# Post-norm pages by halves, kept activation sums, and two more units of the down projection by seven products

## The chip, the core and the metric

The kernel runs on one core of a Trainium2 chip. Its time is the device time of one execution in microseconds. Times of single executions are given as the median of three; the profile is of one more execution, with its own time.

## What is computed

One layer of an encoder block over 256 positions of width 2048, in 32-bit floats. The part that the change touches is the second sub-layer's way out, `@ w_down` and the norm behind it, and the gate that follows:

```python
def conv_glu(hn, w_up, conv_w, conv_b, w_down):
    up = hn @ w_up
    gate, val = jnp.split(up, 2, axis=-1)
    gate = dwconv_centred(gate, conv_w, conv_b)
    return (jax.nn.gelu(gate, approximate=True) * val) @ w_down
...
        mix = jnp.concatenate([y_ssd, y_pool], axis=-1) @ w_out[i]
        h = h + rmsnorm(mix, mix_norm_post[i])
        hn = rmsnorm(h, ffn_norm_pre[i])
        ff = conv_glu(hn, w_ffn_up[i], ffn_conv_w[i], ffn_conv_b[i], w_ffn_down[i])
        h = h + rmsnorm(ff, ffn_norm_post[i])
        gate = jax.nn.sigmoid(rmsnorm(h, ple_norm_pre[i]) @ w_ple_gate[i])
        h = h + rmsnorm(gate * (p[i] @ w_ple[i]), ple_norm_post[i])
```

`w_down` is 5632 x 2048, `w_out` and `w_gate` are 2048 x 2048.

## The kernel before

**Precision.** Every 32-bit operand is split into a high part (a rounding copy on ScalarE, L153) and a low part (the difference, on VectorE, L154); `split` does it for weights, `hid_split` (L962) for the activations of the down projection. A product of two numbers is three matmuls: high by high, high by low and low by high, all 128 x 128 by 128 x 512 (`mm`, L90).

**Stages in order.** The input projections and the state-space and pooling mixers (to about 196 us), the output projection ("wo", to 284 us), a small embedding product ("ple"), the up projection ("ga" and "va", to 785 us), the down projection ("dn", to 1006.6 us), the second half of the embedding product, and the gate ("gt", to the end).

**The sub-layer.** `sublayer` (L854) works "wo" and "dn". It goes through two halves of 1024 output columns. In each, `token_major` (L319) goes through units of two row blocks of 128 of the weight; "dn" has 44 blocks, so 22 units a half. Unit u has the blocks 2u and 2u+1, and tiles are named by the even block and the half: `dn120` is unit 10 of the second half, `dn134` unit 17, `dn18` unit 4, `dn122` unit 11. At the end of a half the accumulators are multiplied by the gain and put aside in two pages `mg` (named `dnm`), one for each 128 positions, taken at the start of the sub-layer; behind the second half they are scaled by the row norm and added to `h` (L883).

**Ordinary and fast units.** An ordinary unit loads 1 MB of weight (`raw`), makes two splits of 1024 columns and issues 24 matmuls. A unit in `dn_fast` is worked by `seven_products` (L269): block products in Strassen's manner, 7 in place of 8, so 21 matmuls. For these it needs sums of weight blocks (a page `t` of 128 x 2048, made by the four additions of `add_blocks`, L263) and sums of activations (`hid_sums`, L1087). Its splits are called `a` (512 columns), `b` (1024, both of the raw weight), `d` and `c` (1024 each, of the page of sums). The products that belong to several output blocks go to separate accumulators (`dn1s`, `dns`), and `combine` (L297) adds them to the main ones (`dna`) one unit after the last fast one; `acc[1][1]`, whose accumulator the text calls dna11_1, is the last of them.

**Where the sums come from.** The weight sums are made ahead, during the up projection: `block_sums` (L227) fetches a raw page (SyncE), adds (VectorE), and stores it to device memory (POOL's queue). A fast unit then loads the page of sums (1 MB, `dn1..t<-dns`) and the last three quarters of the raw weight (768 KB). If no sums are there for a unit, `seven_products` loads the full 1 MB and adds in place, with the splits `a` and `b` ahead. Activation sums of 13 units are made ahead too (`dn_stored`) and loaded by POOL; those of the others are made on the spot in each half: four 128-column operations, a cast, and a 512-column subtraction (`pair_sums`, L818).

**Buffers.** 13 pages of 128 x 2048, 3 raw buffers of the same size, 5 high and 5 low split tiles of 1024 columns, 3 `mid` tiles, 2 activation splits. Loads wait on SyncE for their buffer, and SyncE issues them in its program's order.

**Order.** Only the up projection has its order written out (`in_order`). Elsewhere a scheduler orders the instructions of each engine, so an edit moves instructions that it doesn't name. At unit 11 of the second half, `first` (L1110) loads and splits the gate's first weight (`gtf`, `gtfh`, `gtfl`); at its end `ple_parts` and `back` load the embedding weight and `h`.

Of the kernel before, what the change touches and what calls it, by code (L numbers as in the profile page):

```python
# [11 lines left out]
F32 = mybir.dt.float32  # L12
F32R = mybir.dt.float32r
AF = mybir.ActivationFunctionType
ALU = mybir.AluOpType
ORDERED = (mybir.EngineType.Activation, mybir.EngineType.DVE, mybir.EngineType.SP)

P = 128
# [35 lines left out]
def build(nc, a, out):  # L54
# [3 lines left out]
    w_down, w_gate, w_ple = a["w_down"], a["w_gate"], a["w_ple_"]  # L58
    out = out[0]

    with tile.TileContext(nc) as tc, \
# [9 lines left out]
        def ins(r):  # L71
            return getattr(r, "ins", r)

        def page(name, dtype=F32):
            return gp.tile([P, 2048], dtype, tag="pg", bufs=13, name=name)

        def mid(name, dtype=F32):
            return gp.tile([P, 1024], dtype, tag="mid", bufs=3, name=name)

        def tiny(name, n=2):  # L80
            return sp.tile([P, n], F32, tag="tiny", bufs=40, name=name)
# [35 lines left out]
        def load(dst, src, ahead=False):  # L117

            with tc.issue_after(last["dma"]) if last and not ahead else nullcontext():
                return ins(nc.sync.dma_start(dst, src))  # L120
# [21 lines left out]
        def split(name, src, nel, cuts=()):  # L142

            if name in ready:
                return ready.pop(name)
            if name in spare:
                hi, lo = spare.pop(name)
            else:
                hi = wp.tile([P, 1056], F32R, tag="whi", bufs=5, name=f"{name}h")
                lo = wp.tile([P, 1056], F32R, tag="wlo", bufs=5, name=f"{name}l")  # L150
            for c0, c1 in zip((0, *cuts), (*cuts, nel)):
                s = slice(c0, c1)
                last["act"] = ins(nc.scalar.copy(hi[:, s], src[:, s]))  # L153
                last["dve"] = ins(nc.vector.tensor_sub(lo[:, s], src[:, s], hi[:, s].bitcast(F32)))  # L154
            return hi, lo

        def raw(name, src=None):
            r = wp.tile([P, 2048], F32, tag="raw", bufs=3, name=name)
            if src is not None:
                last["dma"] = load(r, src, True)  # L160
            return r
# [98 lines left out]
            nc.gpsimd.dma_start(t, r)  # L260
            sums_["wo", c * 1024, k] = t, False

        def add_blocks(r):  # L263

            v = r.rearrange("p (b c) -> p b c", b=4)
            for i, j in ((1, 0), (0, 3), (3, 1), (2, 3)):
                nc.vector.tensor_add(v[:, i], v[:, i], v[:, j])  # L267

        def seven_products(name, stage, w, k0, c0, a_, acc, alt, start, stop):  # L269

            if (stage, c0, k0) in sums_:
                r = raw(f"{name}r")
                last["dma"] = load(r[:, 512:], w[c0 // 1024, k0 // 2][:, 512:], True)
                t, held = sums_[stage, c0, k0]
                if not held:
                    t = page(f"{name}t")
                    last["dma"] = load(t, sums_[stage, c0, k0][0], True)
            else:  # L280
                r = t = raw(f"{name}r", w[c0 // 1024, k0 // 2])
            b11 = split(f"{name}a", r[:, 512:1024], 512)
            b2 = split(f"{name}b", r[:, 1024:], 1024)
            if r is t:
                add_blocks(r)
            t42 = split(f"{name}d", t[:, 1024:], 1024)
            t31 = split(f"{name}c", t[:, :1024], 1024)

            for x, (wh, wl), c, o, own in (
                    ("a11", b11, 0, alt[0], True), ("a12", b2, 0, acc[0][0], False), ("a22", t42, 0, acc[1][0], False),  # L290
                    ("s4", b2, 512, acc[0][1], False), ("s2", t42, 512, alt[3], True), ("s1", t31, 512, alt[1], True),
                    ("s3", t31, 0, alt[2], True)):
                xh, xl = a_[x]
                for q, (xx, ww) in enumerate(((xh, wh), (xh, wl), (xl, wh))):
                    mm(o, xx, ww[:, c:c + 512], own and start and q == 0, own and stop and q == 2)
# [175 lines left out]
        for u in range(0, NK, 2):  # L471
            r = [wp.tile([P, 2048], F32, tag="raw", bufs=3, name=f"dtur{u}") if u else r0, page(f"dtur{u + 1}")]
            for j in range(2):
                k = u + j
# [17 lines left out]
            for j in range(2):  # L492
                k = u + j
                with tc.issue_after(front[0]), tc.issue_after(front[1]):
                    wh, wl = split(f"dtu{k}", r[j][:, :1056], 1056, ((352, 704), (704,), (352,))[k] if k < 3 else ())
                if k == 8:
                    half = last["act"], last["dve"]
# [50 lines left out]
        for t in range(2):  # L548
# [3 lines left out]
                                    op0=ALU.mult)  # L552
# [229 lines left out]
        for t in range(2):  # L782
# [13 lines left out]
            r = rms(f"yn{t}", [ss], rz[t][:, 1:2], n=2)  # L796
# [56 lines left out]

        def sublayer(name, w, ks, get, gain, h, vnext, panel=Panel, fast=((), ()), sums=None, at=(), row=None, then=()):  # L854

            mg = [page(f"{name}m{t}") for t in range(2)]
            sq = [[], []]
            for half in range(2):

                alt = main(f"{name}s{half}") if fast[half] and half == 0 else []  # L860
                acc = [main(f"{name}a{half}{t}") for t in range(2)]
                if fast[half]:
                    alt += main(f"{name}s{half}") if half else []
                token_major(f"{name}{half}", w, half * 1024, ks, get, acc, 1, fast[half], alt, sums, at if half else ())
                for t in range(2):
                    for n in range(2):
                        q = tiny(f"{name}q{t}{half}{n}", 1)
                        junk = sp.tile([P, 512], F32, tag="junk", bufs=1, name=f"{name}j{t}{half}{n}")
                        c = slice(half * 1024 + n * 512, half * 1024 + (n + 1) * 512)
                        b = acc[t][n]  # L870
                        if row:
                            nc.scalar.activation(junk, b, AF.Square, scale=row[t], accum_out=q)
                            nc.vector.scalar_tensor_tensor(mg[t][:, c], b, row[t], gain[:, c], op0=ALU.mult, op1=ALU.mult)
                        else:
                            nc.scalar.activation(junk, b, AF.Square, accum_out=q)
                            nc.vector.tensor_mul(mg[t][:, c], b, gain[:, c])
                        sq[t].append(q)
            r = [rms(f"{name}{t}", sq[t], 1.0 / D) for t in range(2)]
            pan = panel(f"{name}x")
            for c in range(4):  # L880
                s = slice(c * 512, (c + 1) * 512)
                for t in range(2):
                    nc.vector.scalar_tensor_tensor(h[t][:, s], mg[t][:, s], r[t], h[t][:, s],  # L883
                                                   op0=ALU.mult, op1=ALU.add)
                panel_part(f"{name}x", pan, h, vnext, 4 * c, 4 * c + 4)
                if c in then:
                    then[c]()
            return pan
# [15 lines left out]
        h = [page(f"h{t}") for t in range(2)]  # L904
# [30 lines left out]
        for t in range(2):  # L935
            h_kept.append(dp.tile([P, D], F32, tag=f"h{t}", bufs=1, name=f"h_kept{t}"))
        pl_kept = dp.tile([P, D], F32, tag="pl", bufs=1, name="pl_kept")

        dn_fast, gt_fast = ((2, 3, 4, 5, 7, 8, 9, 10, 11, 12, 13, 14, 15, 16, 17, 18, 19), (2, 3, 4, 5, 7, 8, 9, 11, 12, 13, 14, 15, 16, 18, 19)), ((4, 5, 6), (1, 2))

        dn_stored = (2, 3, 5, 7, 8, 10, 11, 13, 14, 16, 17, 18, 19)
        gt_ks = list(range(NK)), [0, 1, 8, 9, 10, 11, 2, 3, 4, 5, 6, 7, 12, 13, 14, 15]
        which = [("dn", w_down, c * 1024, 2 * u) for c in range(2) for u in dn_fast[c]] + \
            [("gt", w_gate, c * 1024, gt_ks[c][2 * u]) for c in range(2) for u in gt_fast[c]]
        jobs_at = [[] for _ in range(NPIECES)]

# [3 lines left out]
        for i, w_ in enumerate(which[2:] + which[:2]):  # L950
            fetch, add, store = block_sums(*w_, i >= len(which) - 2)
            n = 46 * i // 10 + 4
# [4 lines left out]
        def hid_part(k):  # L957
            return hid[k // 8][:, (k % 8) * L:(k % 8 + 2) * L]
# [12 lines left out]
        def hid_sums_of(k, s, o):  # L971
            return pair_sums(f"he{k}", s, o, *(hid_part(k)[:, i * P:(i + 1) * P] for i in range(4)))
# [69 lines left out]
        row = norms_row()  # L1042
        with in_order():
            for _ in range(5):
                next_part()
            for n in range(NPIECES):
                s, v, i = blocks[n // 4]
# [32 lines left out]
        def hid_get(k):  # L1080
# [3 lines left out]
                hcache[k0], hcache[k0 + 1] = get_hid(k0), get_hid(k0 + 1)  # L1084
            return hcache[k]

        def hid_sums(k):  # L1087

            (h1, l1), (h2, l2) = get_hid(k), get_hid(k + 1)
            o = mid(f"hd{k}", F32R)  # L1090
            if k in kept:
                nc.gpsimd.dma_start(o.bitcast(F32), kept[k])
                d = sums_in(o)
            else:
                d = hid_sums_of(k, sp.tile([P, 512], F32, tag="junk", bufs=1, name=f"hs{k}"), o)
            return dict(d, a11=(h1[:, :P], l1[:, :P]), a12=(h2[:, :P], l2[:, :P]), a22=(h2[:, P:], l2[:, P:]))

        def ple_parts():
# [73 lines left out]
        for half in range(2):  # L1172
# [12 lines left out]
            for t in range(2):  # L1185
                for n, (o, c0) in enumerate(columns(acc[t])):
                    c1 = c0 + o.shape[-1]
                    c = slice(half * 1024 + c0, half * 1024 + c1)

                    th = mid(f"gth{half}{t}{n}")  # L1190
                    v = th[:, :c1 - c0]
                    end = half == t == 1 and c1 == 1024
                    if end:
# [3 lines left out]
                                                   op0=ALU.add, op1=ALU.mult)  # L1197
# [85 lines left out]
```

## Time and profile before

| | us |
|---|---|
| median of three executions | 1112.9 (1112.57 to 1112.93) |
| the profiled execution | 1113.11 |
| its span in the profile | 1111.3 |
| down, second half, from unit 1 to the end | 900.71 to 1006.56 |
| mean granted clock of TensorE | 0.998 of full speed |

An execution's time has 1.8 us that the span does not hold. Rows of a timeline read: start, duration, engine, line, operation, output <- inputs, shape, count, and in brackets an idle time before it with what ended it. PE is TensorE, DVE is VectorE, ACT is ScalarE, POOL is GpSimd, and SP is SyncE. Durations of neighbouring records on one engine overlap, so the cost of one is read from start to start. Rows of the transfers read: output <- input, queue, count, size, us from issue to landing.

### The profile page before, as it was taken

Reading aid. Unit: us, or ns where it says so; the run is one execution under the profiler, and the core shown is the slowest. Engines: PE = TensorE matmul, PEld = TensorE weight load, DVE = VectorE, ACT = ScalarE, POOL = GpSimd, SP = SyncE. Lnnn points to the kernel's source line nnn. Section 1 sums busy time; section 2 is a strip of 40 time slices with the busy share of each in tenths; the row PEclk is TensorE's granted clock in tenths of the full one; section 3 lists DMA queues with packets and bytes.
Section 4 is the critical chain, followed back from the end, with each engine's and each line's share of the span. In section 5 each row is a group of like instructions: output and inputs, shape, how many; then the busy total and the mean of one; then the engine's idle time right before and its main releaser. Section 6 shows DMA issues by size and latency. Waiting matters only on the chain.

```text
span 1111.3 us, 16096 instructions
## 1 busy us (share of the span) xinstructions
PE 1101.9 (99%) x5961; PEld 951.9 (86%) x5961; DVE 964.0 (87%) x1345; ACT 725.9 (65%) x1059; POOL 78.0 (7%) x143
## 2 busy tenths in 40 slices
PE   9999999999999999999999999999999999999997
PEld 9999988888888888888888888888888888888875
DVE  6589997898868998888888888888899999999995
ACT  6958763555775565665655645657579777877673
POOL 0200000100100000000000000000000000021001
PEclk9999999999999999999999999999999999999999
DMA  9884356555589999999899999999999899996762
GB/s 363 365 330 190 110 194 266 208 218 195 179 347 400 379 396 387 362 367 371 347 378 387 350 383 367 349 392 391 361 382 387 327 344 394 418 392 225 272 242 99
DMA packets 56239, 355.94 MB, mean 320 GB/s; under 512 B 6240, under 2 KB 7136, under 8 KB 20704
## 3 DMA queue, kind: packets, MB, share of 16 engines
q1 hardware_dynamic: 44928, 295.04, 67.9%
q0 software_dynamic: 10800, 59.25, 14.1%
q8 instruction: 47, 0.77, 0.3%
q10 hardware_dynamic: 432, 0.62, 0.2%
q14 instruction: 32, 0.26, 0.1%
HBM read 302.98 MB, written 51.90 MB: 319 GB/s over the span
## 4 chain that ended last, share of the span: by engine, by line
PE 96%; ACT 1%; DVE 1%; issue 1%; POOL 0%; POOLq 0%; ACTq 0%
PE ga L90 22%; PE va L90 22%; PE dna L90 12%; PE woa L90 7%; PE xbc L90 5%; PE gt L90 5%; PE dtu L90 4%; PE z L90 4%; PE dns L90 4%; PE dn0s L90 2%; PE dn1s L90 2%; PE ple L90 1%; PE yd L90 1%; PE gts L90 1%; PE pw L90 1%
## 5 line engine op out<-in xcount | busy, mean ns | idle before, releaser
L90 PE MATMUL ga<-wox,ug_0h 128*128 128x512 f32 x352 | 125.5, 395 | 0.0
L90 PE MATMUL ga<-wox,ug_1h 128*128 128x512 f32 x352 | 125.1, 394 | 0.0
L90 PE MATMUL va<-wox,uv_1h 128*128 128x512 f32 x352 | 124.8, 393 | 0.0
L90 PE MATMUL va<-wox,uv_0h 128*128 128x512 f32 x352 | 124.8, 393 | 0.0
L90 PE MATMUL ga<-wox,ug_1l 128*128 128x256 f32 x352 | 99.1, 282 | 0.0
L90 PE MATMUL va<-wox,uv_1l 128*128 128x256 f32 x352 | 99.1, 281 | 0.0
L90 PE MATMUL va<-wox,uv_0l 128*128 128x256 f32 x352 | 99.1, 281 | 0.0
L90 PE MATMUL ga<-wox,ug_0l 128*128 128x256 f32 x352 | 99.0, 281 | 0.0
L267 DVE TENSOR_TENSOR dnb<-dnb 128x512 f32<-128x512 f32 x128 | 88.3, 690 | 3.1
L90 PEld LDWEIGHTS va<-wox,uv_1h 128*128 128x128 f32 x352 | 66.1, 188 | 15.0
L90 PEld LDWEIGHTS ga<-wox,ug_1h 128*128 128x128 f32 x352 | 66.1, 188 | 15.0 <-DVE wox L191 0.2
L90 PEld LDWEIGHTS va<-wox,uv_0h 128*128 128x128 f32 x352 | 66.1, 188 | 15.0
L90 PEld LDWEIGHTS ga<-wox,ug_0h 128*128 128x128 f32 x352 | 66.1, 188 | 14.8
L90 PEld LDWEIGHTS ga<-wox,ug_0l 128*128 128x128 f32 x352 | 66.2, 188 | 0.1
L90 PEld LDWEIGHTS ga<-wox,ug_1l 128*128 128x128 f32 x352 | 66.2, 188 | 0.0
L90 PEld LDWEIGHTS va<-wox,uv_0l 128*128 128x128 f32 x352 | 66.2, 188 | 0.0
L90 PEld LDWEIGHTS va<-wox,uv_1l 128*128 128x128 f32 x352 | 66.2, 188 | 0.0
L964 ACT CAST hs<-hid 128x512 fp32r<-128x512 f32 x44 | 27.1, 620 | 17.0 <-PE dna L90 16.9
L245 POOL DMA_DIRECT2D dns<-dnb x30 | 16.1, 536 | 311.3 <-DVE dnb L267 298.3
L965 DVE TENSOR_TENSOR hs<-hid,hs 128x512 fp32r<-128x512 f32 x44 | 29.9, 685 | 3.4 <-ACT hs L964 3.4
L826 ACT CAST he<-he 128x512 fp32r<-128x512 f32 x13 | 8.1, 621 | 37.6 <-DVE he L825 37.6
L90 PE MATMUL dna<-dn_0h,hs 128*128 128x512 f32 x96 | 31.2, 393 | 0.0
(2289 smaller groups left out, 3246.4 us busy)
## 6 DMA issues: line engine op xcount, KB each, us to landing
dnb<-w_down SPq DMA_DIRECT2D x32, 1024.0 KB, 9.8
dns<-dnb POOLq DMA_DIRECT2D x30, 1024.0 KB, 7.2
hd<-hsum POOLq DMA_DIRECT2D x24, 512.0 KB, 8.5
zr<-w_z SPq DMA_DIRECT2D x8, 1024.0 KB, 4.9
dtur<-w_dtu SPq DMA_DIRECT2D x14, 528.0 KB, 8.7
dn1r<-w_down SPq DMA_DIRECT2D x7, 1024.0 KB, 8.9
hsum<-he POOLq DMA_DIRECT2D x13, 512.0 KB, 7.4
wo0r<-w_out_ SPq DMA_DIRECT2D x6, 1024.0 KB, 5.0
```

Of the source, the lines that this page charges most:

```text
L90: last["pe"] = ins(nc.tensor.matmul(o, lhsT, rhs, start=start, stop=stop, skip_group_check=True))
L245: nc.gpsimd.dma_start(t, pg[0])
L267: nc.vector.tensor_add(v[:, i], v[:, i], v[:, j])
L826: nc.scalar.copy(o[:, :512], s[:, :512])
L964: nc.scalar.copy(t[:, :512], hid_part(k))
L965: nc.vector.tensor_sub(t[:, 512:], hid_part(k), t[:, :512].bitcast(F32))
```

## The change

Four edits. (1) `sublayer` takes a page for the gain products at the end of each half, and keeps both 128-position parts of a half in it, where it took two pages at its start. (2) `hid_sums` keeps the activation sums that it makes on the spot (units 4, 9, 12, 15) in two pages, and the second half uses them again. (3) Units 10 and 17 of the second half become fast. (4) Units 4, 10 and 17 of the second half are left out of what is made ahead; in "dn" such a unit loads the full raw weight, takes a page and has the block sums written there, ahead of its splits.

```diff
-        def add_blocks(r):
+        APART = ("dn",)
+
+        def add_blocks(r, t=None):

             v = r.rearrange("p (b c) -> p b c", b=4)
-            for i, j in ((1, 0), (0, 3), (3, 1), (2, 3)):
-                nc.vector.tensor_add(v[:, i], v[:, i], v[:, j])
+            s = v if t is None else t.rearrange("p (b c) -> p b c", b=4)
+            for i, a, b in ((1, v, 0), (0, v, 3), (3, s, 1), (2, s, 3)):
+                nc.vector.tensor_add(s[:, i], v[:, i], a[:, b])
...
                 r = t = raw(f"{name}r", w[c0 // 1024, k0 // 2])
+                if stage in APART:
+                    t = page(f"{name}t")
+                    add_blocks(r, t)
             b11 = split(f"{name}a", r[:, 512:1024], 512)
...
-            mg = [page(f"{name}m{t}") for t in range(2)]
+            mg = []
...
                 token_major(f"{name}{half}", w, half * 1024, ks, get, acc, 1, fast[half], alt, sums, at if half else ())
+                mg.append(page(f"{name}m{half}"))
...
+                        m = mg[half][:, t * 1024 + n * 512:t * 1024 + (n + 1) * 512]
...
-                            nc.vector.scalar_tensor_tensor(mg[t][:, c], b, row[t], gain[:, c], op0=ALU.mult, op1=ALU.mult)
+                            nc.vector.scalar_tensor_tensor(m, b, row[t], gain[:, c], op0=ALU.mult, op1=ALU.mult)
...
-        dn_fast, gt_fast = ((2, 3, 4, 5, 7, 8, 9, 10, 11, 12, 13, 14, 15, 16, 17, 18, 19), (2, 3, 4, 5, 7, 8, 9, 11, 12, 13, 14, 15, 16, 18, 19)), ((4, 5, 6), (1, 2))
-
+        dn_fast, gt_fast = ((2, 3, 4, 5, 7, 8, 9, 10, 11, 12, 13, 14, 15, 16, 17, 18, 19), (2,3,4,5,7,8,9,10,11,12,13,14,15,16,17,18,19)), ((4, 5, 6), (1, 2))
+
+        dn_here = (), (4,10,17,)
...
-        which = [("dn", w_down, c * 1024, 2 * u) for c in range(2) for u in dn_fast[c]] + \
+        which = [("dn", w_down, c * 1024, 2 * u) for c in range(2) for u in dn_fast[c] if u not in dn_here[c]] + \
...
+        own, own_pages = {}, []
+
         def hid_sums(k):

             (h1, l1), (h2, l2) = get_hid(k), get_hid(k + 1)
-            o = mid(f"hd{k}", F32R)
             if k in kept:
+                o = mid(f"hd{k}", F32R)
                 nc.gpsimd.dma_start(o.bitcast(F32), kept[k])
                 d = sums_in(o)
             else:
-                d = hid_sums_of(k, sp.tile([P, 512], F32, tag="junk", bufs=1, name=f"hs{k}"), o)
+                if k not in own:
+                    n = len(own)
+                    if n % 2 == 0:
+                        own_pages.append(page(f"hd{k}", F32R))
+                    own[k] = hid_sums_of(k, sp.tile([P, 512], F32, tag="junk", bufs=1, name=f"hs{k}"),
+                                         own_pages[-1][:, n % 2 * 1024:(n % 2 + 1) * 1024])
+                d = own[k]
```

In the orders that result, the program has 6 matmuls and 8 VectorE instructions fewer, and SyncE's queue in the second half asks for 120r, 122r, 124r, the gate's first page, 126r, 122t, 124t, 126t, where it asked for 120's raw weight, the gate's first page, 122r, 124r, 122t, 124t, 126r, 126t.

More of the change, by code (lines that the diff above doesn't have):

```diff
@@ L872, in sublayer @@
                             nc.scalar.activation(junk, b, AF.Square, scale=row[t], accum_out=q)
-                            nc.vector.scalar_tensor_tensor(mg[t][:, c], b, row[t], gain[:, c], op0=ALU.mult, op1=ALU.mult)
+                            nc.vector.scalar_tensor_tensor(m, b, row[t], gain[:, c], op0=ALU.mult, op1=ALU.mult)
                         else:
                             nc.scalar.activation(junk, b, AF.Square, accum_out=q)
-                            nc.vector.tensor_mul(mg[t][:, c], b, gain[:, c])
+                            nc.vector.tensor_mul(m, b, gain[:, c])
                         sq[t].append(q)
@@ L882, in sublayer @@
                 for t in range(2):
-                    nc.vector.scalar_tensor_tensor(h[t][:, s], mg[t][:, s], r[t], h[t][:, s],
+                    m = mg[c // 2][:, t * 1024 + c % 2 * 512:t * 1024 + (c % 2 + 1) * 512]
+                    nc.vector.scalar_tensor_tensor(h[t][:, s], m, r[t], h[t][:, s],
                                                    op0=ALU.mult, op1=ALU.add)
```

## The prediction

> **What bounds the kernel now.** I read the page's busy times and its chain of waits first, then the table by windows over the second half of the down projection, where the edits fall, and then the timelines of TensorE, VectorE, ScalarE and SyncE at the two units that become fast.
>
> ```profile
> span 1111.3 us, 16096 instructions
> ...
> PE 1101.9 (99%) x5961; PEld 951.9 (86%) x5961; DVE 964.0 (87%) x1345; ACT 725.9 (65%) x1059; POOL 78.0 (7%) x143
> ...
> PE 96%; ACT 1%; DVE 1%; issue 1%; POOL 0%; POOLq 0%; ACTq 0%
> ```
>
> TensorE works through 1101.9 of 1111.3 us and holds 96% of the chain that ends last. So a matmul taken out should come off the end, if everybody else keeps up. VectorE, at 87% on the mean, is the next in line, so the stage has to be looked at by itself.
>
> ```profile
> core 0: us, PE busy (x) PEld busy (x) DVE busy (x) ACT busy (x) POOL busy (x), PEclk, DMA share, GB/s
> 900.71:1006.56 105.85, 105.85 (x460) 86.12 (x459) 100.85 (x124) 81.74 (x103) 12.67 (x14) 1.00 0.96 385
> 900.71:945.69 44.98, 44.98 (x196) 36.59 (x195) 42.71 (x56) 35.76 (x44) 2.15 (x4) 1.00 0.98 386
> 939.25:1003.23 63.98, 63.98 (x279) 52.10 (x278) 60.53 (x72) 50.05 (x61) 9.56 (x7) 1.00 0.96 392
> ```
>
> The first row is the second half of down from unit 1 to its end: TensorE never stops there, at 105.85 / 460 = 0.2301 us a matmul and the full clock. But VectorE is busy 100.85 of 105.85 us, and the DMA engines move 385 GB/s at a share of 0.96. Three resources are nearly full in the stage that the change rearranges; the last row shows that from unit 9's second splits to the end VectorE has 3.45 us free.
>
> **What the change takes from TensorE.** Units 10 and 17 go from 24 matmuls to 21 each. The order of instructions shows 6 fewer for the program: 6 x 0.2301 = 1.38 us. If TensorE stays gap-free, the profiled execution of 1113.11 us (1111.3 of span and 1.8 around it) becomes 1111.7.
>
> **What it does to VectorE.**
>
> ```profile
> 770.44 2.87 DVE L267 TENSOR_TENSOR dnb<-dnb 128x512 f32<-128x512 f32 x4
> 773.23 1.22 DVE L154 TENSOR_TENSOR uv_0l<-uv101r,uv_0h 128x1024 fp32r<-128x1024 f32 x1
> ...
> 937.51 0.69 DVE L154 TENSOR_TENSOR dn118al<-dn118r,dn118ah 128x512 fp32r<-128x512 f32 x1
> 938.11 1.22 DVE L154 TENSOR_TENSOR dn118bl<-dn118r,dn118bh 128x1024 fp32r<-128x1024 f32 x1
> ...
> 940.05 1.23 DVE L154 TENSOR_TENSOR dn118dl<-dn118t,dn118dh 128x1024 fp32r<-128x1024 f32 x1 [0.72 <-ACT dn118dh L153]
> 941.19 1.22 DVE L154 TENSOR_TENSOR dn118cl<-dn118t,dn118ch 128x1024 fp32r<-128x1024 f32 x1
> ...
> 945.20 2.35 DVE L154 TENSOR_TENSOR gtfl<-gtf,gtfh 128x1024 fp32r<-128x1024 f32 x2
> ...
> 949.81 0.68 DVE L827 TENSOR_TENSOR hd<-hs,hd 128x512 fp32r<-128x512 f32 x1
> 950.53 0.29 DVE L822 TENSOR_TENSOR hs<-hid 128x128 f32<-128x128 f32 x1
> 950.74 0.28 DVE L823 TENSOR_TENSOR hs<-hid 128x128 f32<-128x128 f32 x1
> ...
> 1002.54 0.69 DVE L317 TENSOR_TENSOR dna<-dna,dn1v 128x512 f32<-128x512 f32 x1
> 1003.14 1.22 DVE L154 TENSOR_TENSOR ple_0l<-ple1r,ple_0h 128x1024 fp32r<-128x1024 f32 x1
> ```
>
> The prices are read from start to start, since records overlap: 0.60 us for 512 columns (937.51 to 938.11), 1.135 for 1024 (half the 2.27 from gtfl at 945.20 to the next instruction at 947.47), 0.205 for 128. Block sums cost 2.4 if each takes 0.60, and 2.79 as the four in a row show (770.44 to 773.23).
>
> Added in this half: three units' block sums, 3 x (2.4 to 2.8); and two units whose splits grow from 2 x 1.135 to 0.60 + 3 x 1.135, or 2 x 1.735. Removed: four units' activation sums, each 4 x 0.205 + 0.60 = 1.42. Net 7.2 + 3.5 - 5.7 = +5.0 us in a stage with 5.0 free. It is not evenly spread. In the stretch to 945.69 unit 4's sums are paid for by the activation sums of units 4 and 9 (2.4 to 2.8 against 2.84), with 2.3 us free besides: no cost. From unit 9 on, two units bring 2 x (2.4 + 1.735) = 8.3, and only 2.0 goes: the row at 949.81 (unit 12's), and four small subtractions from 950.53 with the 0.60 behind them (unit 15's).
>
> I count this stretch in the two orders, from the start of 118d (118bl's start at 938.11 + 1.135 = 939.25) through the last combine, dna11_1, the addition at 1002.54. Before: 36 of 1024, 30 of 512 and 4 of 128, so 59.7 us, and it ended at 1003.14 with 4.2 of waits. After: 38 of 1024 and 37 of 512 (the last unit's activation split moves behind the combine), so 38 x 1.135 + 37 x 0.60 = 65.3. Without any wait dna11_1 is done at 939.25 + 65.3 + 0.1 (record over pitch) = 1004.7; with the adds at 0.70 it is 1005.4. It cannot start earlier by much: the split pools hold five tiles and a fast unit takes four, so VectorE works about one unit ahead and no more. The 0.72 us wait at 940.05 is covered in the new order, where a split and an add come first.
>
> The page "VectorE: DVE Perf Modes" of the Trainium skill, section "The DRAIN you can't avoid", says that a vector operation starts only when the pipe of the one before is empty, save for those not held. By it each of the 75 operations would take its whole record, some 0.085 us more, and the sum would be 6.4 higher. The rows at 937.51 and 938.11 are 0.60 apart with a 0.69 record, so the exception holds here for splits; only the four chained adds (0.70 each) come near the rule.
>
> ```profile
> 945.69 0.62 PE L90 MATMUL dna<-dn_0h,hs 128*128 128x512 f32 x2
> 951.24 0.39 PE L90 MATMUL dns<-dn122ah,hs 128*128 128x512 f32 x1
> 1001.03 0.39 PE L90 MATMUL dna<-dn_0h,hs 128*128 128x512 f32 x1
> 1005.18 0.39 PE L90 MATMUL dna<-dn_0h,hs 128*128 128x512 f32 x1
> 1006.56 0.39 PE L90 MATMUL ple<-ple_0h,pth 128*128 128x512 f32 x1
> ```
>
> These are the starts of unit 10, unit 11, the last unit (21), its first product into the accumulator dna11_1, and the embedding product behind it. In the old order that product comes 18 matmuls into the unit, at 1005.18, 2.0 us after the addition. In the new order 10 matmuls come first. Gap-free, unit 21 starts at 1001.03 - 1.38 = 999.65 and TensorE wants dna11_1 at 999.65 + 10 x 0.2301 = 1001.95. VectorE gives it at 1004.7: **a wait of 2.7 us**, up to 3.5 with the dearer adds, which turns the gain into +1.3 to +2.1. Where along the half TensorE pays makes no difference to the end.
>
> **The loads that move.**
>
> ```profile
> 949.08 1.05 ACT L153 CAST dn122dh<-dn122t 128x1024 fp32r<-128x1024 f32 x1 [1.09 <-DMA dn122t<-dns]
> ...
> 939.36 0.33 SPq L120 DMA_DIRECT2D dn124r<-w_down  x1
> 939.74 0.43 SPq L120 DMA_DIRECT2D dn122t<-dns  x1
> 940.22 0.42 SPq L120 DMA_DIRECT2D dn124t<-dns  x1
> ...
> dn14t<-dns SPq DMA_DIRECT2D x1, 1024.0 KB, 7.4
> dn16r<-w_down SPq DMA_DIRECT2D x1, 768.0 KB, 5.0
> ...
> dn122t<-dns SPq DMA_DIRECT2D x1, 1024.0 KB, 9.2
> ```
>
> SyncE issues in program order. Before, unit 11's block sums (122t) are asked for at 939.74, land 9.2 us later, and even so the cast waits 1.09. Afterwards 126r stands in front of 122t, 124t and 126t, and 126r must wait for the raw buffer of unit 10, which is free when VectorE has done 120bl. The new VectorE order from 939.25 is a 512 split, add, 118d, 118c, two adds, 120a, add, 120b: 6 x 0.60 + 3 x 1.135 = 7.0, so 946.3. 122t follows at about 946.7 and, at the 7.4 of 14t (a load of the same kind that also follows a 768 KB one by 0.4), lands at 954.1. The cast takes 1.05, so with 0.1 of signalling VectorE can start 122d at 955.2. It gets there 7.4 after 946.3 (two activation splits, 120d, 120c, both gtfl, 122a, 122b), at 953.7: **1.5 us late**, and the chain above has no slack, so it counts in full. Bounds: landing in 5.0 there is no wait (and no gain); in 9.2 it is 3.3. I take 7.4 since the queue then holds the 126r ahead and little else of that age. Unit 10's raw load grows from 768 KB plus a 1 MB page to 1 MB alone; the two more small activation loads go through POOL, 7% busy. ScalarE loses four casts.
>
> The page "DMA: Bandwidth & Descriptors", section "Anatomy of one DMA", fits 2.0 us and bytes over 436 GB/s for GpSimd-issued transfers; estimated from it, 126r and 122t together land 6.2 us after the first is issued, which would cut the wait to 0.3 and the forecast by 1.2. No run shows that path alone here.
>
> **The rest.** Gain products in pages by halves, same instructions, another page: 0; a page less is held in the first half, and the first half has no TensorE gap to win back (its share of the chain is TensorE's). The kept sums of four units hold two pages instead, again 0 unless a page comes late, which is in the range. One precomputation less (a fetch, four adds, a store) is hidden in the up projection, where TensorE is also gap-free: 0. At the exit to the gate one more split of 1.135 stands among the gain products:
>
> ```profile
> 1011.76 0.88 DVE L191 SCALAR_TENSOR_TENSOR dnxl<-dnxt,vt,dnxh 128x256 fp32r<-128x256 f32 x2 [0.20 <-ACT dnxh L190]
> 1012.55 1.22 DVE L154 TENSOR_TENSOR gt_0l<-gt0r,gt_0h 128x1024 fp32r<-128x1024 f32 x1
> ...
> 1013.02 0.63 PE L90 MATMUL gt<-gtfh,dnxh 128*128 128x512 f32 x2
> ...
> 1065.54 0.50 PE L90 MATMUL gt<-gt18bl,dnxh 128*128 128x512 f32 x1 [0.44 <-DVE gt18bl L154]
> ```
>
> It used to follow the panel's first low parts. Their high parts are there by 1011.76 and are first used at 1013.02, some 1.2 us later, which covers the 1.135 about once: 0 to 0.5, and I take 0.2.
>
> Sum: 1113.11 - 1.38 + 2.7 + 1.5 + 0.2 = 1116.1. The median of the runs shown, 1112.9, is 0.2 below the profiled execution: **1115.9 us**.
>
> **The rivals.** (A, forecast) VectorE is the bound of the second half and one load comes late. Its own range goes from no late load, cheap adds (1114.4) to late load 3.3 and wait 3.5 with 0.5 at the exit (1118.8).
>
> (B) VectorE bounds, but 122t is in time, as 16r's 5.0 us allows: 1115.9 - 1.5 = 1114.4. Against it stands the 1.09 wait of today, with a load asked for 7 us earlier in the order; for it, the fewer loads in flight.
>
> (C) The cover holds, the other side: not slower. VectorE's waits of today are only the price of being ahead, and it would have to make 4.2 us of waits vanish and another 2.7 appear as lead, from unit 9 to 21. It decides if dna11_1 is done by 1001.95. Then only the six matmuls count: 1111.7, on the median 1111.5. If the gate's 0.44 gap shrinks as well, 1111.1. Against it: 65.3 us of starts do not fit into 62.7.
>
> (D) The late load is as slow as today's 122t (9.2 us): 3.3 in place of 1.5 and adds at 0.70: 1115.9 + 1.8 + 0.8 = 1118.5. For it speaks the DMA share of 0.96, and unit 17, which repeats unit 10's pattern with a full raw load that has to be there before the adds.
>
> **How the numbers follow.** A 0.48, B 0.24, C 0.12, D 0.16. A measurement of this kernel tells 0.2%, 2.2 us, from no change: below 1110.7 is faster, above 1115.1 slower. A gives slower 0.43 and the same 0.05, B the same 0.22 and slower 0.02, C the same 0.07 and faster 0.05 (other gaps of the gate going too), D slower 0.16. So faster 0.05, the same 0.34, slower 0.61. The range runs from 1112.4 (C left out, B's lower part in) to 1118.8 (A's and D's upper ends).
>
> **What would show it.** TensorE gaps of 2 to 5 us in all between units 10 and 21, ended by VectorE's low parts or by dna11_1 (in C: none). In the window from unit 9 on, VectorE busy without its 3.45 us of free time. 126r issued at about 946.3, 122t landing near 954, and the cast 122dh waiting on DMA; B if it does not. Unit 4 without a gap. The up projection the same to 0.3 us. The forecast is wrong if VectorE enters unit 10 more than 1 us earlier against TensorE than today, if SyncE's order on the chip keeps 122t early, or if a page wait appears before unit 9.

## The result, and the profile after

The changed kernel takes 1117.44 us in the median of six executions (1115.37 to 1119.19), the kernel before 1112.81 (1112.55 to 1112.97): a ratio of 1.0041, with a 95% interval of 1.0031 to 1.0052. The forecast was 1115.9 with 1112.4 to 1118.8. The executions also scatter nine times as widely as before. The profiled one took 1118.01.

The page of the changed kernel, first the span and the busy times, then the chain of waits by engine:

```profile
span 1116.2 us, 16073 instructions
...
PE 1102.8 (99%) x5955; PEld 949.2 (85%) x5955; DVE 966.0 (87%) x1337; ACT 727.8 (65%) x1059; POOL 88.1 (8%) x144
...
PE 91%; DVE 4%; ACT 2%; issue 1%; DMA 1%; POOL 0%; POOLq 0%; SPq 0%; ACTq 0%; DVEq 0%
```

Six matmuls are gone, and 5% of the chain has passed from TensorE to others. Where, the windows of the second half show (the same stretches and columns as before):

```profile
900.71:1006.56 105.85, 102.46 (x437) 81.03 (x436) 99.93 (x113) 80.07 (x97) 20.97 (x12) 1.00 0.94 370
900.71:945.69 44.98, 44.98 (x196) 36.45 (x195) 41.49 (x48) 33.27 (x41) 2.70 (x5) 1.00 0.91 341
...
939.25:1003.23 63.98, 60.59 (x256) 47.09 (x255) 61.55 (x71) 50.12 (x61) 18.81 (x8) 1.00 0.96 382
```

To 945.69 TensorE still runs without a gap, unit 4 with its sums on the spot included. From then on it has gaps, and VectorE is left 2.43 us without work, in spite of being late. The timelines of VectorE, ScalarE and SyncE name that time:

```profile
950.31 2.36 DVE L154 TENSOR_TENSOR gtfl<-gtf,gtfh 128x1024 fp32r<-128x1024 f32 x2 [1.09 <-ACT gtfh L153]
...
956.36 1.22 DVE L154 TENSOR_TENSOR dn122dl<-dn122t,dn122dh 128x1024 fp32r<-128x1024 f32 x1 [1.34 <-ACT dn122dh L153]
...
1006.70 0.69 DVE L323 TENSOR_TENSOR dna<-dna,dn1v 128x512 f32<-128x512 f32 x1
...
949.24 1.99 ACT L153 CAST gtfh<-gtf 128x1024 fp32r<-128x1024 f32 x2 [1.91 <-DMA gtf<-w_gate]
951.13 0.61 ACT L153 CAST dn122ah<-dn122r 128x512 fp32r<-128x512 f32 x1
...
955.28 1.05 ACT L153 CAST dn122dh<-dn122t 128x1024 fp32r<-128x1024 f32 x1 [2.06 <-DMA dn122t<-dns]
...
939.74 0.49 SPq L120 DMA_DIRECT2D gtf<-w_gate  x1
946.38 0.33 SPq L120 DMA_DIRECT2D dn126r<-w_down  x1
946.76 0.43 SPq L120 DMA_DIRECT2D dn122t<-dns  x1
```

1.09 + 1.34 = 2.43: two transfers. One is 122t, asked for behind 126r at 946.76. The other is the gate's page, asked for at 939.74 behind 124r; ScalarE, which works in program order, waits 1.91 us for it with 122ah behind. So TensorE's gaps begin earlier than forecast:

```profile
951.80 0.50 PE L90 MATMUL dns<-dn122ah,hs 128*128 128x512 f32 x1 [1.08 <-ACT dn122ah L153]
952.75 0.50 PE L90 MATMUL dna<-dn122bh,hs 128*128 128x512 f32 x1 [0.44 <-ACT dn122bh L153]
...
956.38 0.50 PE L90 MATMUL dna<-dn122dh,hs 128*128 128x512 f32 x1 [0.71 <-ACT dn122dh L153]
...
1007.45 0.50 PE L90 MATMUL dna<-dn_0h,hs 128*128 128x512 f32 x1 [0.45 <-DVE dna L323]
...
1011.83 0.40 PE L90 MATMUL ple<-ple_0l,pth 128*128 128x512 f32 x1
```

Measured from start to start, over the 0.23 of a matmul, TensorE loses about 4.4 us at unit 11, 0.9 at unit 17 and 0.8 at unit 21: 6.1 against 1.4 saved. The prediction had named gaps of 2 to 5 us in all.

### The profile page after: what moved, and what is told of

Same layout as the page of the kernel before. It is cut to its first block, busy times and chain, and to the rows that moved or that the text cites. A ratio compares the mean times of both kernels' runs of the same rounds, so it can differ in the third digit from the quotient of the medians.

```text
span 1116.2 us, 16073 instructions
## 1 busy us (share of the span) xinstructions
PE 1102.8 (99%) x5955; PEld 949.2 (85%) x5955; DVE 966.0 (87%) x1337; ACT 727.8 (65%) x1059; POOL 88.1 (8%) x144
## 4 chain that ended last, share of the span: by engine, by line
PE 91%; DVE 4%; ACT 2%; issue 1%; DMA 1%; POOL 0%; POOLq 0%; SPq 0%; ACTq 0%; DVEq 0%
PE ga L90 22%; PE va L90 22%; PE dna L90 9%; PE woa L90 7%; PE xbc L90 5%; PE gt L90 5%; PE dtu L90 4%; PE z L90 4%; PE dns L90 3%; PE dn0s L90 2%; PE ple L90 1%; PE dn1s L90 1%; DMA dn122t<-dns 1%; PE yd L90 1%; PE gts L90 1%
## 5 line engine op out<-in xcount | busy, mean ns | idle before, releaser
L270 DVE TENSOR_TENSOR dnb<-dnb 128x512 f32<-128x512 f32 x124 | 85.6, 690 | 3.1
L1104 POOL DMA_DIRECT2D hd<-hsum x26 | 14.1, 540 | 219.1 <-PE dn0s L90 90.2
```

Of the source, the lines that this page charges most:

```text
L270: nc.vector.tensor_add(s[:, i], v[:, i], a[:, b])
```

## The experiments

Medians of each kernel; the ratio is to executions of the kernel before on the same chip (whose medians were 1112.71, 1113.04 and 1113.01 in the three series of four).

| run | us | ratio, 95% interval |
|---|---|---|
| gate_load_early | 1114.87 | 1.0021 (1.0013 to 1.0030) |
| gate_at_7 | 1120.22 | 1.0068 (1.0055 to 1.0080) |
| sums_stored | 1115.31 | 1.0025 (1.0015 to 1.0035) |
| sums_on_gpsimd | 1123.20 | 1.0095 (1.0082 to 1.0109) |
| ten_ordinary | 1112.89 | 1.0001 (0.9992 to 1.0010) |
| seventeen_ordinary | 1116.70 | 1.0033 (1.0021 to 1.0044) |
| pages_and_kept_sums | 1112.82 | 0.9999 (0.9990 to 1.0008) |
| early_load_17_stored | 1115.01 | 1.0018 (1.0010 to 1.0027) |
| st17_copy_late | 1114.33 | 1.0013 (1.0005 to 1.0022) |
| act_order_at_17 | 1115.30 | 1.0022 (1.0013 to 1.0032) |
| only_17_stored | 1115.00 | 1.0019 (1.0011 to 1.0028) |
| sums_stored_copy_late | 1114.78 | 1.0015 (1.0006 to 1.0024) |

### The late loads against VectorE's work: gate_load_early

```diff
+        def first_load():
+
+            cur["gtf"] = page("gtf")
+            last["dma"] = load(cur["gtf"], w_gate[0, 0])
+
         def first():
 
-            r, hi, lo = page("gtf"), page("gtfh", F32R), page("gtfl", F32R)
-            last["dma"] = load(r, w_gate[0, 0])
+            r, hi, lo = cur.pop("gtf"), page("gtfh", F32R), page("gtfl", F32R)
...
-                      fast=dn_fast, sums=hid_sums, at={11: first, NF // 2: lambda: (ple_parts(), back())}, row=rf, then={1: lambda: second(0), 2: lambda: second(1)})
+                      fast=dn_fast, sums=hid_sums, at={8: first_load, 11: first, NF // 2: lambda: (ple_parts(), back())}, row=rf, then={1: lambda: second(0), 2: lambda: second(1)})
```

> The changed kernel, but the load of the gate's first page is issued at unit 8 in place of unit 11; its splits stay at unit 11. SyncE's order is then gate page before 116r, and 122t, 124t before 126r. VectorE's work and its place stay. Theory V+L (VectorE bounds, two late loads add): the waits of 1.9 us (gtfh) and 2.1 us (122dh) on DMA in ScalarE go, the VectorE chain from 939.25 to dna11_1 runs without a wait and ends near 1004.7, TensorE waits about 2.7 us in unit 21 and hardly at unit 11; time 1117.4 - 2.7 = 1114.7 (1114.2 to 1115.5). Rival L (late loads alone are the cost): no TensorE wait is left, 1111.5 to 1112.5. Rival V (VectorE alone, loads are hidden by its lateness): 1117 unchanged.

1114.87 came out where the two causes together gave 1114.7; late loads alone (1111.5 to 1112.5) and VectorE alone (1117) fall. Here are, for this kernel, the VectorE rows at both ends of the chain, the window from the subtraction behind 118bl to dna11_1, and TensorE's waits:

```profile
937.36 1.22 DVE L154 TENSOR_TENSOR dn118bl<-dn118r,dn118bh 128x1024 fp32r<-128x1024 f32 x1
938.49 0.69 DVE L975 TENSOR_TENSOR hs<-hid,hs 128x512 fp32r<-128x512 f32 x1
...
1003.34 0.69 DVE L323 TENSOR_TENSOR dna<-dna,dn1v 128x512 f32<-128x512 f32 x1
...
938.49:1003.34 64.85, 63.13 (x271) 50.03 (x269) 64.85 (x76) 50.81 (x62) 19.45 (x8) 1.00 0.97 387
...
951.39 0.50 PE L90 MATMUL dns<-dn122al,hs 128*128 128x512 f32 x1 [0.76 <-DVE dn122al L154]
...
980.90 0.50 PE L90 MATMUL dna<-dn134bh,hs 128*128 128x512 f32 x1 [0.44 <-ACT dn134bh L153]
...
982.60 0.50 PE L90 MATMUL dna<-dn134dh,hs 128*128 128x512 f32 x1 [0.52 <-ACT dn134dh L153]
...
1004.09 0.50 PE L90 MATMUL dna<-dn_0h,hs 128*128 128x512 f32 x1 [0.44 <-DVE dna L323]
```

VectorE is busy 64.85 of 64.85 us. The chain takes 1003.34 + 0.69 - 938.49 = 65.5; counted ahead, it was 65.3 + 0.1. With no load late, TensorE still loses 3.5 us from start to start, and VectorE has not a moment free. One detail was otherwise: TensorE waits at units 11 (1.0), 17 (1.6) and 21 (0.8), not in one piece at the end. The wait for the cast 134bh at unit 17 is ScalarE's; a run below takes it away.

### The gate's split moved too: gate_at_7

```diff
-                      fast=dn_fast, sums=hid_sums, at={11: first, NF // 2: lambda: (ple_parts(), back())}, row=rf, then={1: lambda: second(0), 2: lambda: second(1)})
+                      fast=dn_fast, sums=hid_sums, at={7: first, NF // 2: lambda: (ple_parts(), back())}, row=rf, then={1: lambda: second(0), 2: lambda: second(1)})
```

> The changed kernel, but the gate's first page is loaded and split at unit 7, behind the ordinary unit 6, and not at unit 11. Both late loads go as above and 2.27 us of VectorE's chain behind 939.25 move to a place with free time. V+L: chain 65.3 - 2.3 = 63.0, dna11_1 at 1002.4, TensorE waits 0.5 us; time 1112.0 to 1113.0. L: 1111.5 to 1112.5, the same as with the load alone moved. V: the gain over the changed kernel is 2.3 us at most, 1115. If two pages held from unit 7 make the pages short, loads of 116t or 118t come late and the time is above 1114.

It is the slowest but one of all kernels, and over 7 us above the range expected, though 2.27 us of VectorE's work left the tight stretch. SyncE's order had changed again; its rows, ScalarE's and TensorE's:

```profile
925.69 0.33 SPq L120 DMA_DIRECT2D dn118r<-w_down  x1
926.07 0.42 SPq L120 DMA_DIRECT2D dn114t<-dns  x1
...
934.34 1.04 ACT L153 CAST dn114dh<-dn114t 128x1024 fp32r<-128x1024 f32 x1 [2.39 <-DMA dn114t<-dns]
...
935.44 0.50 PE L90 MATMUL dna<-dn114dh,hs 128*128 128x512 f32 x1 [2.07 <-ACT dn114dh L153]
```

114t, the next page needed, now stands behind 118r, which waits for a raw buffer until 925.69. It is the same fault as 122t behind 126r, further ahead in the half. The expectation had named late loads of 116t or 118t, for want of pages, as what would spoil it; it was 114t, behind a raw load. TensorE loses 2.8 us there. VectorE waits 2.7 us there for 114dh, more than the 2.27 that were moved away, so it comes no earlier to the tight stretch, and TensorE loses about 3.8 us more at units 10, 17 and 21. What the moved work is worth by itself this run doesn't show.

### One unit at a time: ten_ordinary, seventeen_ordinary, pages_and_kept_sums

```diff
-        dn_fast, gt_fast = ((2, 3, 4, 5, 7, 8, 9, 10, 11, 12, 13, 14, 15, 16, 17, 18, 19), (2,3,4,5,7,8,9,10,11,12,13,14,15,16,17,18,19)), ((4, 5, 6), (1, 2))
-
-        dn_here = (), (4,10,17,)
+        dn_fast, gt_fast = ((2, 3, 4, 5, 7, 8, 9, 10, 11, 12, 13, 14, 15, 16, 17, 18, 19), (2,3,4,5,7,8,9,11,12,13,14,15,16,17,18,19)), ((4, 5, 6), (1, 2))
+
+        dn_here = (), (4,17)
```

> The changed kernel with unit 10 of the second half ordinary again; units 4 and 17 fast with sums on the spot. SyncE's order around unit 11 is that of before (gate page ahead of 122r, 122t ahead of 126r). V+L (VectorE's sum of work and the two late loads): no wait at unit 11; VectorE's chain behind 939.25 is 65.3 - 4.1 = 61.2, done at 1000.5, ahead of TensorE's 1002.6; left are the 0.7 to 1.4 us at unit 17, where TensorE waits for 134dh behind its block sums, against 3 matmuls (0.69) saved: 1112.0 to 1113.5. If kept sums or pages cost something by themselves, more.

The second run leaves 17 out in the same way, with `dn_here = (), (4, 10)`; the third both, with `dn_here = (), ()`.

> The changed kernel with unit 17 of the second half ordinary again; units 4 and 10 fast with sums on the spot. SyncE's order around unit 11 is that of the changed kernel. V+L: the TensorE waits at unit 11 stay (4.4 us in all), none at units 17 and 21: 1112.7 - 0.7 + 4.4 = 1116.4 (1115.5 to 1117.5). By VectorE's sum of work alone (61.2 behind 939.25) there would be no wait: 1112.0.

> Only the first two edits: gain products in pages by halves and the kept activation sums; units 10 and 17 ordinary, and all block sums made ahead as before. Forecast by the prediction: both cost nothing, 1112.7 (1112.3 to 1113.1); VectorE's second half 5.7 us less busy and no TensorE wait. If pages come short, a wait on a page of sums and more.

All three fell inside their ranges. The pages by halves and the kept sums cost nothing and bring nothing (0.9999), although VectorE then works only 94.75 us of the half in place of 100.85:

```profile
900.71:1006.56 105.85, 105.85 (x460) 85.91 (x459) 94.75 (x104) 79.75 (x100) 14.88 (x13) 1.00 0.95 377
```

Units 4 and 17 on top cost nothing measurable (ten_ordinary). Its one TensorE wait, 0.8 us, is at dna11_1 and not at unit 17: the count of work without waits had that addition done at 1000.5, but VectorE waited 0.72 us ahead of 118dl and 0.76 ahead of 122dl, and it was done at 1002.15. Unit 10 carries the loss: with units 4 and 10 and without 17 the time is 1116.7, though by the count VectorE's work would be done in time. At unit 11 of that kernel (seventeen_ordinary) ScalarE waits on the same two transfers:

```profile
948.19 2.00 ACT L153 CAST gtfh<-gtf 128x1024 fp32r<-128x1024 f32 x2 [1.49 <-DMA gtf<-w_gate]
...
953.77 1.05 ACT L153 CAST dn122dh<-dn122t 128x1024 fp32r<-128x1024 f32 x1 [1.60 <-DMA dn122t<-dns]
```

TensorE loses 3.4 us at unit 11 there, in the fastest of its six executions, and nothing at units 17 and 21. Not all of this is the loads: in gate_load_early, where no load is late, 1.0 us is lost at unit 11 to VectorE's 122al. A sum of work up to the end of the half doesn't show such a place within it. An ordinary unit 10 had been the place in which the gate's page could be loaded and split.

### Taking the additions off VectorE: sums_stored, sums_on_gpsimd

```diff
-        dn_here = (), (4,10,17,)
+        dn_here = (), ()
...
-            n = 46 * i // 10 + 4
+            n = 44 * i // 10 + 4
```

> The changed kernel, but no block sums on the spot: those of units 4, 10 and 17 are made ahead too and stored, with two more jobs spread over the up projection (every 4.4 pieces in place of 4.6). VectorE's second half loses 12 adds, 7.2 us, 8 of them (4.8 us) behind 939.25; the transfers of the half grow by 3 x 0.75 MB net, about 6 us of the 385 GB/s seen. V+L: dna11_1 at 1004.7 - 4.8 = 999.9, ahead of TensorE's 1001.95, so no wait there; 1111.5 to 1112.5 if the loads come in time. If the transfers bound (D): waits on the pages of sums, 1114 to 1118.

```diff
-                nc.vector.tensor_add(s[:, i], v[:, i], a[:, b])
+                (nc.vector if t is None else nc.gpsimd).tensor_add(s[:, i], v[:, i], a[:, b])
```

> The changed kernel with the block sums of units 4, 10 and 17 added on GpSimd. No run so far shows the price of a 128x512 addition there. V+L: VectorE's chain is 4.8 us shorter behind 939.25, dna11_1 near 1000 to 1001, no TensorE wait from VectorE; 1111.5 to 1113 if an addition takes under 2 us. If it takes more, 120dh waits for the sums and unit 10 stalls by four times the excess; if VectorE's own operations get slower while GpSimd adds (seen as longer starts to starts than 0.60 and 1.135), 1113 to 1116.

With the sums stored, VectorE has 4.0 us free between 940 and 1000, and the time is 1115.3 all the same. The same window of the changed kernel, and then of this one, shows what is full now:

```profile
940.00:1000.00 60.00, 56.61 (x239) 43.84 (x238) 57.57 (x64) 47.99 (x60) 18.21 (x7) 1.00 0.96 381
```

```profile
940.00:1000.00 60.00, 59.12 (x247) 44.99 (x246) 56.02 (x61) 48.76 (x60) 6.08 (x8) 1.00 1.02 417
```

ScalarE waits for transfers ten times and 7.9 us in all in this half, and the time lies in the range that the expectation gave for transfers as the bound. How much of it they cost isn't shown by this run: of the 3.7 us that TensorE loses, 2.2 lie behind 991, where another cause is at work too (the next section). A fast unit with stored sums moves 1.75 MB in 4.83 us and an ordinary one 1 MB in 5.55; in the ordinary units the transfers can catch up.

On GpSimd the additions cost most of all: 1123.20 lies above every range that was given. For that kernel, VectorE's rows and GpSimd's:

```profile
940.57 1.79 DVE L975 TENSOR_TENSOR hs<-hid,hs 128x512 fp32r<-128x512 f32 x1
942.29 2.32 DVE L154 TENSOR_TENSOR dn118dl<-dn118t,dn118dh 128x1024 fp32r<-128x1024 f32 x1
944.53 2.30 DVE L154 TENSOR_TENSOR dn118cl<-dn118t,dn118ch 128x1024 fp32r<-128x1024 f32 x1
...
948.45 1.22 DVE L154 TENSOR_TENSOR dn120bl<-dn120r,dn120bh 128x1024 fp32r<-128x1024 f32 x1
...
940.30 3.22 POOL L270 TENSOR_TENSOR dn120t<-dn120r 128x512 f32<-128x512 f32 x2 [1.98 <-DMA dn120r<-w_down]
943.48 4.50 POOL L270 TENSOR_TENSOR dn120t<-dn120r,dn120t 128x512 f32<-128x512 f32 x2
```

An addition takes 1.6 to 2.25 us here, and VectorE's 1024-column splits 2.3 in place of 1.22 meanwhile. From 940.57 to 948.45 VectorE works two splits of 512 columns and two of 1024: 7.9 us for what takes 3.5 otherwise. The four additions cost it 4.4 us where they saved 2.4.

### A miss and what lay behind it: early_load_17_stored, st17_copy_late, sums_stored_copy_late

The kernel of gate_load_early with `dn_here = (), (4, 10)`:

> The kernel with the gate's page loaded at unit 8, and unit 17's block sums made ahead and stored, so that only units 4 and 10 add on the spot. V+L: VectorE's chain is 65.3 - 2.4 = 62.9, dna11_1 near 1002.3, TensorE waits 0.3 us there and not at unit 17; the 0.9 us at 122al stays: 1112.8 - 1.4 + 1.2 = 1112.6 (1112.0 to 1113.5), between the kernel before and the one with the load moved alone (1114.9). By transfers (0.75 MB more at a share of 0.95): as slow as with all sums stored, 1115.

It took 1115.01 and not 1112.6, the time that the expectation gave for transfers as the bound. Yet transfers weren't it: ScalarE waits for them 0.2 us in all. This kernel's ScalarE and VectorE show another order:

```profile
990.81 0.59 ACT L310 COPY dn1v<-dns 128x512 f32<-128x512 f32 x1 [1.44 <-PE dns L90]
991.29 1.05 ACT L153 CAST dn138dh<-dn138t 128x1024 fp32r<-128x1024 f32 x1
...
992.37 1.23 DVE L154 TENSOR_TENSOR dn138dl<-dn138t,dn138dh 128x1024 fp32r<-128x1024 f32 x1 [2.09 <-ACT dn138dh L153]
```

The combine's first copy waits for TensorE's last product into `dns`, and the cast that TensorE needs next is queued behind it. Behind 991 TensorE loses 2.4 us (1.9 of it before 1000), about as much as was missed. The last two kernels move that copy, in this one and in the one with all sums stored:

```diff
-            nc.scalar.copy(p1, alt[0])
+            with tc.issue_after(last["act"]) if name == "dn1" else nullcontext():
+                nc.scalar.copy(p1, alt[0])
```

> The kernel with the gate's page loaded at unit 8 and unit 17's sums stored (1115.0), and in it the first copy of the second half's combine (dn1v from dns, on ScalarE) is put behind the casts of unit 20, where it stood ahead of the casts 138dh and 138ch and waited 1.44 us for TensorE's last product into dns. Theory Q (ScalarE's order cost the 2.5 us missed): 138dh is cast when its page lands, near 989.5, VectorE's 2.1 us of idle time ahead of 138dl goes, the TensorE waits after 991 (1.9 us in all) go; 1113.1 (1112.6 to 1113.7), the 0.9 us at unit 11 stays. Rival D (transfers bound with 0.75 MB more): 138dh waits for its page instead, 1114.5 to 1115.2.

> The kernel with all block sums stored (1115.3), with the combine's first copy behind unit 20's casts. ScalarE waited 7.9 us for transfers there in all, and 0.5 for the copy's product. D (transfers bound when 2.25 MB more are to be moved): the waits for pages stay, 1114.5 to 1115.5. Q: 1113.5 or less.

In the first, the row of ScalarE shows the wait gone:

```profile
989.10 1.05 ACT L153 CAST dn138dh<-dn138t 128x1024 fp32r<-128x1024 f32 x1
```

TensorE's gaps behind 991 shrink from 2.4 us to 0.9. The median moves by 0.7, to 1114.33, between the two ranges of the expectation, and the two intervals overlap: the wait was there, but taking it away is not shown to pay. What was won is lost in part behind the half, where TensorE's gaps grow from 3.7 to 4.6 us. The largest of the new ones, 0.5 us in the gate, is a wait for ScalarE's scaling of the embedding product, and all three kernels with the copy moved have it. With all sums stored the waits for transfers remain (4.6 us) and the time, 1114.78, is inside the range of the transfers.

### Does unit 17 count by itself: act_order_at_17

The kernel of gate_load_early; at the place that is changed, `last["b2"]` is the cast 134bh, and `early_hs` serves to pick the second half:

```diff
             b2 = split(f"{name}b", r[:, 1024:], 1024)
+            last["b2"] = last["act"]
...
             t = lp.tile([P, 1024], F32R, tag="hs", bufs=2, name=f"hs{k}")
-            nc.scalar.copy(t[:, :512], hid_part(k))
+            early_hs[-k - 1] = -k - 1 in early_hs
+            with tc.issue_after(last["b2"]) if k == 36 and early_hs[-k - 1] else nullcontext():
+                nc.scalar.copy(t[:, :512], hid_part(k))
```

> The kernel with the gate's page loaded at unit 8 (1114.9), and in it the cast of unit 18's activations, which waited 2.3 us for its buffer on ScalarE ahead of the casts 134ah and 134bh, is put behind 134bh. V+L (VectorE's chain ends the half): the TensorE wait of 0.7 us for 134bh goes, that for 134dh stays or shrinks, and what is won at unit 17 is waited for at dna11_1 in unit 21, since VectorE has no idle time from 940 to 1000: 1114.9 (1114.5 to 1115.2), dna11_1 near 1004.0 again. Rival Q (ScalarE's order at unit 17 sets the end): 1114.2.

The wait for 134bh is gone, and TensorE waits for 134dh instead (1.2 us in place of 0.7). 1115.30 lies just above the range given, and the ratio is the same as without the edit, 1.0022 against 1.0021. With VectorE busy 60.00 of the 60 us from 940 to 1000, ScalarE's order at unit 17 is worth nothing.

### A version to beat both: only_17_stored

The kernel of ten_ordinary with `dn_here = (), (4,)` and the copy moved:

> A version that could beat both: unit 10 ordinary as before, unit 17 fast with its sums made ahead and stored, unit 4 on the spot, pages and kept sums as changed, the gate's page at unit 11 as ever, and the combine's first copy behind unit 20's casts. Three matmuls fewer (0.69). V+L: VectorE's chain behind 939.25 is 61.2 - 2.4 = 58.8, no wait for it; 1112.7 - 0.7 = 1112.0 (1111.7 to 1112.5). D (0.75 MB more in a full stage): waits for pages, 1113 or more.

1115.00, between 1113.42 and 1118.00 in eleven executions: a miss. In the profiled one (1114.21) ScalarE waits 2.6 us for 122t, and TensorE's gaps come to 1.1 us in the half and 4.6 behind it, where it was 4.0 before; the executions near 1118 have no profile. That transfers come late in them is a guess from the 0.75 MB more, and isn't shown. No kernel of the series beats the one before.

## Why the prediction held, and where it didn't

**The matmuls**: six fewer, 1.38 us, as worked out.

**VectorE's sum**: right in size. The chain, counted as 65.3 us from two orders and three prices, took 65.5 where no load disturbed it, and cost TensorE 3.5 us where the sum had 2.7. More than half of the difference is a miscount: 8 matmuls, six of unit 21 and two of the embedding product, come ahead of dna11_1 in the new order, and the sum had 10. Two matmuls are 0.46 us. That VectorE's work alone costs this much rests on its full window and on a count made ahead of the run; no kernel here takes work off VectorE and leaves all else as it was, since the runs that tried also delayed a load, added transfers or slowed VectorE.

**The loads**: 126r was issued at 946.38, where 946.3 was worked out. VectorE's wait ahead of 122dl was 1.34 where the sum had 1.5, but this is luck: 122t took 8.4 us from issue to landing and not 7.4, so that its cast began at 955.28 and not near 954.2, and VectorE too came there about a microsecond later than forecast. The step that was too small is the sentence that put VectorE at 122d "at 953.7", with both gtfl in between as if the gate's page were there. It had moved behind 124r to 939.74, took 9.5 us to land, its cast began only at 949.24, and VectorE lost 1.09 more. Both loads together cost 1117.44 - 1114.87 = 2.6 us, where the sum had 1.5.

Two readings in that part were wrong without weight for the sum. Unit 10 was ordinary before and loaded 1 MB then as now; only unit 4's loads shrink. And an estimate of 6.2 us for 126r and 122t, counted from 126r's issue at 946.3 as it says, leaves no wait at all and not 0.3; measured from there, 122t landed after 8.8 us.

The terms as the traces show them: -1.4 for the matmuls, 3.5 for TensorE's waits without late loads (gate_load_early), 2.6 for what the late loads add (6.1 - 3.5), and 0.1 at the exit to the gate, where the sum had 0.2. (From the embedding product behind the half to the end it is 104.37 us, with two products of 0.23 moved ahead of it, against 104.74 before.) Together they are 4.8, against 4.6 between the medians, 4.9 between the profiled executions, and 3.0 forecast.

**"Where along the half TensorE pays makes no difference"**: right for the time, but the place was not unit 21 alone. ScalarE's queue was left out: TensorE's first wait was for 122ah, a cast with its data long there (asked for at 934.75, landed after 6.8 us), behind the gate's cast. Nor did ScalarE "lose four casts" on balance: the splits of units 10 and 17 bring four, and its count is 1059 before and after.

**The rivals**: B is what gate_load_early shows (1114.4 forecast, 1114.87). C fell with VectorE's window full. Of D's two sources neither decided: 122t's 8.4 us lie between the 7.4 of the sum and D's 9.2, and unit 17's full raw load was in time, since VectorE went from 132cl to the additions without a wait.

**At no cost**: pages, kept sums, unit 4's sums and the dropped precomputation were worth nothing either way, as said.

## What to carry to other kernels

Where the busiest engine is fed by one that is 95% full, count the feeder's starts over the tight stretch in the new order: three prices and two instruction lists gave the chain to 0.2 us in the kernel in which it ran without a wait. Look at places within the stretch too: at unit 11 TensorE waited for VectorE long before the end. Then go through every queue that works in program order, SyncE's loads and ScalarE's casts: in four kernels here (the changed one, gate_at_7, seventeen_ordinary and early_load_17_stored) an entry that waited for a buffer, a page or a product stood ahead of one that was ready, or of the load needed next, and TensorE lost 1.5 to 3.4 us there. An ordinary unit among fast ones is not only slow; here it gave VectorE, the transfers and the queues room that the fast ones use up.

## What was not expected of the hardware

While GpSimd's additions run, VectorE's subtractions are slower, both with two operands in on-chip memory: 2.3 us for 1.22, and 1.79 for 0.69. The Trainium skill, "SBUF — State Buffer", section "Who interferes with whom", says that a VectorE instruction with two such inputs contends with a GpSimd instruction that reads that memory; the rows agree, and put the price at 1.9 to 2.6 times. Whether the additions are slowed too isn't shown: no run has one beside an idle VectorE.

In the same run, 1 us behind a TensorE gap of 2.1 us (950.75 to 953.13, less a matmul), eight matmuls came 0.43 us apart, in windows with a granted clock of 0.54 and 0.61:

```profile
954.00:956.00 2.00, 2.00 (x7) 1.59 (x6) 2.00 (x4) 2.00 (x3) 0.00 (x0) 0.54 1.00 418
956.00:958.00 2.00, 2.00 (x7) 1.58 (x6) 2.00 (x3) 0.64 (x2) 0.00 (x0) 0.61 0.93 378
```

The eight cost 1.6 us more than at 0.23. In gate_at_7 a gap of as much, 2.2 us (932.97 to 935.44, less a matmul), was followed by a granted clock of 1.00. Whether the gap brought the slow clock, and what decides, isn't shown. The clock may also have a part in the changed kernel's scatter: of its six executions the two slowest, 1119.19 and 1118.89, have the lowest mean granted clocks, 0.995 and 0.996, and the others 0.997 and 0.998; that too isn't shown.
